# Nearest 2x upsampling: the first 52 rows of every partition taken from a block of their own in DRAM

## The chip, the core and the metric

The kernel runs on one core of a Trainium2 chip. The metric is the device time of one execution in microseconds. Before the change the median of three runs is 197.23 us (197.15 to 197.36).

## What is computed

The input `x` is float32 of shape (16, 64, 64, 64). Every value is written four times: each row of 64 becomes a row of 128 by doubling every element, and each of these rows is written twice.

```
for i in range(new_h):
    for j in range(new_w):
        result[:, :, i, j] = x[:, :, i // scale_factor, j // scale_factor]
```

No arithmetic takes place. 16.78 MB come in and 67.11 MB go out, 83.89 MB in all.

## The kernel before

**Rows.** The three leading dimensions are taken together: 65,536 rows of 64 floats (256 B). Each of the 128 partitions has 512 of them, one after another in DRAM (`xp`, L173), so that partition p starts 128 KiB after partition p-1. The output is cut in the same way: an input row makes 256 floats (1 KiB), and a partition has 512 KiB (`op`, L174).

**Memory.** One buffer `mem` (L187) holds everything: in each partition a free stretch of 79 x 256 floats, and behind it the 512 rows of the input (`xt`). The expanded groups of rows are written by turns at the start of the buffer and at a place that ends in the rows of `xt` already used (L208).

**Loads.** Four transfers on SyncE's queue (L195) bring rows 0 to 32, 32 to 256, 256 to 480 and 480 to 512 of every partition. They are the first instructions of SyncE, moved ahead of the start barrier by `begin_before_barrier`, and wait for nothing. Call them load 0 to load 3.

**Groups.** The rows are worked on in nine groups of 52, 40, 52, 63, 52, 64, 63, 63 and 63 rows (L181). Of each group VectorE copies 9/16 (L215) and ScalarE the rest (L216), both with an input pattern that repeats every element and every row. Then SyncE issues one store for the group (L217). Call them store 0 to store 8. VectorE's part of the first group is rows 0 to 29, ScalarE's is rows 29 to 52; load 0 therefore serves VectorE alone, and ScalarE waits for load 1.

**What sets the order.** All 13 transfers go through one queue, in the order in which SyncE issues them. Store 0 has an extra wait by hand: for load 2 (`loads[-2]`, L221), so that the stores begin as the loads end, while load 3 still runs. From the third group on a group's copies wait until the store two before it has left its place in `mem`.

`close_early` rewrites the end of the program, so that SyncE's last instruction is the wait for the last store.

Of the kernel before, what the change touches and what calls it, by code (L numbers as in the profile page):

```python
# [153 lines left out]
@with_exitstack  # L154
def kernel(
    ctx: ExitStack,
    tc: tile.TileContext,
    x: bass.AP,
    scale_factor: int,
    out: bass.AP,  # L160
):
    nc = tc.nc
    nc.at_finalize(begin_before_barrier)
    nc.at_finalize(close_early)
    P = nc.NUM_PARTITIONS
    s = int(scale_factor)
    B, C, H, W = x.shape
    R = B * C * H // P
    fdt = x.dtype

    xp = x.rearrange("b c h w -> (b c h) w").rearrange("(p r) w -> p r w", p=P)  # L173
    op = out.rearrange("b c (h hd) w -> (b c h) (hd w)", hd=s).rearrange(  # L174
        "(p r) w -> p r w", p=P
    )

    rows = [52, 40, 52, 63, 52, 64, 63, 63, 63]  # L181
    GROW = s * s
    FREE = 79
    WF = FREE * GROW * W
    assert sum(rows) == R
    mem_pool = ctx.enter_context(tc.tile_pool(name="mem", bufs=1))
    mem = mem_pool.tile([P, WF + R * W], fdt, name="mem")  # L187
    xt = mem[:, WF:].rearrange("p (r w) -> p r w", r=R)

    HEAD = 32
    cuts = [0, HEAD, R // 2, R - 32, R]
    loads = [
        nc.sync.dma_start(out=xt[:, lo:hi], in_=xp[:, lo:hi])  # L195
        for lo, hi in zip(cuts, cuts[1:])
    ]

    def expanded(r0, r1):
        return (  # L200
            xt[:, r0:r1].unsqueeze(2).unsqueeze(4).to_broadcast([P, r1 - r0, s, W, s])
        )

    r0 = 0
    before = (0, 0)
    for n, k in enumerate(rows):
        size = k * GROW * W
        at = 0 if n % 2 == 0 else WF + r0 * W - size  # L208
        assert at >= before[1] or at + size <= before[0]
        before = (at, at + size)  # L210
        u = mem[:, at : at + size].rearrange(
            "p (k a w b) -> p k a w b", k=k, a=s, w=W
        )
        kv = k * 9 // 16
        nc.vector.tensor_copy(out=u[:, :kv], in_=expanded(r0, r0 + kv))  # L215
        nc.scalar.copy(out=u[:, kv:], in_=expanded(r0 + kv, r0 + k))  # L216
        store = nc.sync.dma_start(out=op[:, r0 : r0 + k, :], in_=u)  # L217
        if n == 0:
            tc.add_manual_dep(
                store.ins,  # L220
                loads[-2].ins.name,  # L221
                mybir.DependencyInfo(
                    mybir.DependencyClass.Sync, mybir.DependencyReason.DATA
                ),
                reason="stores begin as the loads end",
            )
        r0 += k
# [35 lines left out]
```

## Time and profile before

| what | value |
|---|---|
| median of three runs | 197.23 us |
| the profiled execution, its own time | 197.0 us |
| its span, first to last instruction | 195.7 us |
| outside the span | 1.3 us |
| transfers | 13, in 1872 packets |
| VectorE busy | 69.7 us (36%) |
| ScalarE busy | 51.4 us (26%) |
| load 0 landed, by VectorE's first copy | 4.59 us |
| load 1 landed, by its second copy | 21.52 us |
| load 2 landed, by the chain | 38.44 us |

The span is counted from SyncE's first instruction. A transfer is cut into packets, and 16 DMA engines move them at the same time; the DMA share is the mean busy share of these engines. A short window's GB/s is rough, since whole packets are put where they start.

In the views "mem<-in_x_dram" is a load, "out_dram<-mem" a store, "mem<-mem" a copy, SPq is SyncE's queue, and "L215" is a line of the kernel.

### The profile page before, as it was taken

What the parts mean: (1) busy time and instruction counts of PE and PEld (TensorE: products, weight loads), DVE (VectorE), ACT (ScalarE), POOL (GpSimd) and SP (SyncE); (2) the same over time, 40 slices, a digit from 0 to 9 for tenths busy, and PEclk for the clock granted to TensorE, in tenths of its full rate; (3) what the DMA queues carried; (4) which work ended last, traced back from release to release, by engine and by line L of the source; (5) the groups of instructions that cost most, each with busy time, mean ns of one, the idle gap of its engine ahead of it and who ended that gap; (6) DMA issues with size and microseconds to landing.
All of it is one profiled execution on the core that took longest, in us unless ns stands there. A gap on an engine that the chain in (4) does not pass through costs nothing.

```text
span 195.7 us, 105 instructions
## 1 busy us (share of the span) xinstructions
DVE 69.7 (36%) x9; ACT 51.4 (26%) x10; POOL 0.2 (0%) x4
## 2 busy tenths in 40 slices
DVE  0950600000039299069008205930692079100000
ACT  0000595000036093064910006666000074000000
POOL 0000000000000000000000000000000000000000
DMA  9899889799899989899999899999999999999994
GB/s 402 375 481 457 375 375 563 310 440 523 348 442 452 526 348 512 359 422 422 422 422 523 348 523 429 429 429 429 422 422 422 422 422 422 528 514 422 435 422 211
DMA packets 1872, 83.89 MB, mean 429 GB/s; under 512 B 208, under 2 KB 208, under 8 KB 208
## 3 DMA queue, kind: packets, MB, share of 16 engines
q1 hardware_dynamic: 1872, 83.89, 99.3%
HBM read 16.78 MB, written 67.11 MB: 429 GB/s over the span
## 4 chain that ended last, share of the span: by engine, by line
DMA 67%; DVE 18%; SPq 0%; issue 0%; DVEq 0%
DMA out_dram<-mem 48%; DMA mem<-in_x_dram 19%; DVE mem L215 18%; SPq L195 0%; DVEq L215 0%; SPq L217 0%
## 5 line engine op out<-in xcount | busy, mean ns | idle before, releaser
L215 DVE COPY mem<-mem 128x8960 f32<-128x8960 f32 (+3 forms) x9 | 69.7, 7740 | 97.5 <-DMA out_dram<-mem 83.9
L216 ACT COPY mem<-mem 128x7168 f32<-128x7168 f32 (+2 forms) x9 | 50.1, 5572 | 90.8 <-DMA out_dram<-mem 84.3
L216 ACT ACT_TABLE_LOAD x1 | 1.3, 1283 | 21.6 <-DMA mem<-in_x_dram 21.6
L244 POOL MEMSET const-bfloat16-1.0<- 128x1 bf16 x1 | 0.1, 102 | 0.0
L244 POOL MEMSET const-uint8-127<- 128x1 uint8 x1 | 0.1, 102 | 0.0
L244 POOL MEMSET const-float32-0.0<- 128x1 f32 x1 | 0.1, 99 | 0.2 <-issue 0.2
L244 POOL MEMSET const-float32-1.0<- 128x1 f32 x1 | 0.1, 99 | 0.0
## 6 DMA issues: line engine op xcount, KB each, us to landing
out_dram<-mem SPq DMA_DIRECT2D x4, 8064.0 KB, 28.4
out_dram<-mem SPq DMA_DIRECT2D x3, 6656.0 KB, 19.7
mem<-in_x_dram SPq DMA_DIRECT2D x2, 7168.0 KB, 29.3
out_dram<-mem SPq DMA_DIRECT2D x1, 5120.0 KB, 29.8
mem<-in_x_dram SPq DMA_DIRECT2D x2, 1024.0 KB, 22.1
out_dram<-mem SPq DMA_DIRECT2D x1, 29.9
```

Of the source, the lines that this page charges most:

```text
L215: nc.vector.tensor_copy(out=u[:, :kv], in_=expanded(r0, r0 + kv))
L216: nc.scalar.copy(out=u[:, kv:], in_=expanded(r0 + kv, r0 + k))
L244: nc = _bacc.Bacc("TRN2", target_bir_lowering=False, num_devices=1)
```

## The change

Input and output are each cut into two blocks. The first block is the first 128 x 52 rows of `x` (1.70 MB in one piece), 52 for each partition; the second is the rest, 460 rows for each partition. A partition's rows 0 to 52 now come from the first block and its rows 52 to 512 from the second, and the output is cut alike. Load 0 brings 52 rows instead of 32, and load 1 204 instead of 224.

```diff
-    xp = x.rearrange("b c h w -> (b c h) w").rearrange("(p r) w -> p r w", p=P)
-    op = out.rearrange("b c (h hd) w -> (b c h) (hd w)", hd=s).rearrange(
-        "(p r) w -> p r w", p=P
-    )
+    HEAD = 52
+    xf = x.rearrange("b c h w -> (b c h) w")
+    of = out.rearrange("b c (h hd) w -> (b c h) (hd w)", hd=s)
+
+    def blocks(flat):
+        return (
+            flat[: P * HEAD].rearrange("(p r) w -> p r w", p=P),
+            flat[P * HEAD :].rearrange("(p r) w -> p r w", p=P),
+        )
+
+    def rows_of(parts, lo, hi):
+        if hi <= HEAD:
+            return parts[0][:, lo:hi]
+        assert lo >= HEAD
+        return parts[1][:, lo - HEAD : hi - HEAD]
+
+    xp, op = blocks(xf), blocks(of)
...
-    HEAD = 32
     cuts = [0, HEAD, R // 2, R - 32, R]
     loads = [
-        nc.sync.dma_start(out=xt[:, lo:hi], in_=xp[:, lo:hi])
+        nc.sync.dma_start(out=xt[:, lo:hi], in_=rows_of(xp, lo, hi))
         for lo, hi in zip(cuts, cuts[1:])
     ]
...
-        store = nc.sync.dma_start(out=op[:, r0 : r0 + k, :], in_=u)
+        store = nc.sync.dma_start(out=rows_of(op, r0, r0 + k), in_=u)
```

The distance from one partition's rows to the next partition's changes thus:

| | before | first block | second block |
|---|---|---|---|
| input | 131,072 B | 13,312 B | 117,760 B |
| output | 524,288 B | 53,248 B | 471,040 B |

A row of load 0 or of store 0 now ends where the next partition's begins. The nine groups, the copies, the place of each group in `mem` and the wait of store 0 for load 2 stay.

## Prediction

> **What bounds the kernel now.** I began with the page's first three parts, to see who is busy. VectorE works 36% of the span and ScalarE 26%, and the DMA engines never rest:
>
> ```profile
> DMA  9899889799899989899999899999999999999994
> ...
> DMA packets 1872, 83.89 MB, mean 429 GB/s; under 512 B 208, under 2 KB 208, under 8 KB 208
> ## 3 DMA queue, kind: packets, MB, share of 16 engines
> q1 hardware_dynamic: 1872, 83.89, 99.3%
> ```
>
> The reader is to see the 99.3%: the 16 engines are occupied for all of the span but about 1.4 us of 195.7. The same view, asked for the stretch from 1.02 us (the first packet) to 195.28 us (the last packet's end), says where that rest lies:
>
> ```profile
> q1 hardware_dynamic: 1872, 83.89, 100.0%
> ```
>
> So there is no gap inside: 1.02 us pass before the first packet and 0.4 us after the last. That also says how to read the chain that ended last, which names VectorE for 18%:
>
> ```profile
> 0.91 37.52 DMA mem<-in_x_dram
> ...
> 38.52 18.23 DMA out_dram<-mem
> ...
> 56.85 7.90 DVE mem L215
> ...
> 64.83 19.72 DMA out_dram<-mem
> ```
>
> The chain follows one transfer at a time. While VectorE copies from 56.85 to 64.75 us, store 1, which was queued behind store 0, keeps the engines at work; the copies are covered. What counts is bytes by pace, and so I read the pace in windows (the last column is GB/s):
>
> ```profile
> 0.90:3.90 3.00, 0.00 (x0) 0.00 (x0) 0.00 (x0) 1.00 0.98 347
> 3.90:20.90 17.00, 7.88 (x1) 0.00 (x0) 0.00 (x0) 1.00 1.01 436
> 20.90:37.90 17.00, 3.09 (x1) 10.41 (x3) 0.00 (x0) 1.00 1.00 432
> 119.30:157.60 38.30, 18.97 (x2) 12.31 (x2) 0.00 (x0) 1.00 1.00 434
> ```
>
> Two things matter here. Loads, whose partitions lie 128 KiB apart, go at 434 GB/s (mean of 436 and 432); stores, whose partitions lie 512 KiB apart, go at 434 too. A fourfold distance and the opposite direction give one pace, so neither sets it. And only the first 3 us are slower, at 347.
>
> At 434 GB/s one input row of all 128 partitions (32,768 B) takes 0.0755 us and its output row (131,072 B) 0.302 us. 512 of both make 193.3 us. The other 2.4 us of the span are the start and the end: 1.02 before the first packet, 0.4 after the last, and some 0.5 in the first load (0.60 us by the window, 3.00 x 87/434, of which 0.12 lie before 1.02 us; by single packet records, the 128 packets of load 0 last 368 ns in the mean and the equal packets of load 3 last 310, so 8 per engine x 58 ns = 0.47). What is left, 0.5 us or 0.3%, is about as much as windows of this kind are rough by.
>
> **The change, part by part.**
>
> *Load 0 grows from 32 to 52 rows.* It landed at 4.59 us; 20 rows more at 0.0755 are 1.51, so 6.1 us. VectorE's first copy (7.88 us) then runs from 6.1 to 14.0 instead of 4.6 to 12.5. Its next copy waits for load 1, which ends with row 256 in both kernels and so lands at 21.5 as before: 7.5 us of cover are left. On the path: 0. If load 1 came before 14.0, the delay would show in VectorE, and still not at store 0, see next.
>
> *ScalarE's first copy needs load 0 only.* It waited 21.6 us for load 1. Now its table load (1.28) and copy (5.10) run from 6.1 to 12.5, and its second copy (4.03) from 21.5 to 25.5, where the old pair ended at 32.0. That takes 6.5 us off ScalarE's work ahead of stores 0 and 1. SyncE held store 0 for another reason:
>
> ```profile
> SPq L217 <- DMA mem<-in_x_dram: 36.1, 1, 36.1
> ```
>
> This is the hand-made wait for load 2, which ended at 38.44, 6.4 us after ScalarE was done. The slack grows to 12.9 us and is worth 0. What covers the issue of store 0 at 38.52 is load 3, whose 32 rows keep the engines busy for 2.4 us; that row range and its place in the queue are unchanged.
>
> *Load 1 shrinks from 224 to 204 rows.* The sum of loads 0 and 1 is 256 rows in both. Transfers stay 13, and if each keeps 128 pieces (1872 less 208 small packets is 1664, 13 x 128), the packet costs stay. 0.
>
> *No wait is added*, no queue is passed by another, and stores 1 to 8 keep their order and their buffers. The tightest cover afterwards is that of store 2, issued at 64.8 while store 1 lands at about 68.8: 4 us. 0, unless a store gets slower by that.
>
> *The distances change.* This is the only part that can touch the path, and the trace shows no transfer with the new distances. Bounds:
> - Steady pace, gain side: 0, since engines that are 100.0% busy move 434 GB/s in both directions at two distances, which is a ceiling of theirs and not of an address pattern.
> - Steady pace, loss side: the slowest pace in the trace, 347 GB/s, for the block that lies in one piece. Load 0 (1.70 MB): 4.91 against 3.93 us, +0.98, less the 0.60 that is paid now, so +0.4. Store 0 (6.82 MB): 19.6 against 15.7, +3.9. Together +4.3. I take 0, from the rows nearest by far: 34 us of loads and 38 us of stores without a slow stretch.
> - Start of load 0: the 0.47 us lie mostly in the first packet of each engine (728 ns against 309 over the first 16 packets). Gain at most 0.47, if 16 engines that start together hinder each other because of the 128 KiB distance. Loss 0.29, if the excess grows with the bytes (0.47 x 20/32). I take -0.1: it sits in the first packet and so is mostly waiting for first data, which another distance doesn't remove.
>
> **A rule against the trace.** The Trainium skill, page "DMA: Bandwidth & Descriptors", section "Latency and other measured facts", speaks for the change: copies between DRAM tensors whose rows lie 512 KiB apart gave 207 GB/s per direction, and an uneven distance 214. An estimate by it takes 3.3% off the stores' 154.6 us, so -5.1 us. The stores' row above, 434 GB/s at 512 KiB, disagrees, and the same page's "Where 436 GB/s comes from" gives 435 as the ceiling of the ports. I go by the row.
>
> **Sum.** 195.7 - 0.1 = 195.6 us of span; with 1.3 outside, 196.9 for the profiled execution. That execution (197.0) lay 0.23 under the median, so the forecast for the median is 197.23 - 0.1 = **197.1 us**. A measurement of this kernel can tell about 0.2%, 0.39 us, from no change.
>
> **The rivals.**
> 1. *The block in one piece has a slower pace.* Sixteen engines that read or write rows 13 or 52 KB apart work in one small stretch of DRAM, and may hinder each other there. For: the only slow stretch of the trace is one where all engines start together in short rows. Against: the last load has the same short rows and isn't slow. Price: +0.4 (load alone) to +4.3 us (with store 0), so 197.6 to 201.5. It decides as soon as the pace over load 0 and store 0 (19.6 us at 434) falls by 2%, below 425 GB/s. Slower.
> 2. *The start gets quick.* The 0.47 us of the first packets vanish, because the engines no longer begin 128 KiB apart: 196.8 us, 0.24% faster. For: a first packet alone would not take 2.4 times its later time in all 16 engines unless something is shared. Against: waiting for first data needs no collision. More is hardly to be had, for the rest of the span is 100.0% busy at one pace.
> 3. *It doesn't do what it says:* a piece of DRAM without gaps is cut otherwise than into 128 rows, and fewer engines share it. At half of them load 0 and store 0 take 3.9 + 15.7 = 19.6 us more: 216.8 us. Nothing in the profile speaks for it; all 13 transfers of before have 128 pieces, but none of them lay in one piece.
>
> **Chances.** Forecast (within 0.2%) 0.58; rival 1, 0.24; rival 2, 0.14; rival 3, 0.04. So faster 0.14, same 0.58, slower 0.28. The range takes in the forecast and rival 2, hence 196.7 below. Above it may leave out 2 in 10: rival 3 and two thirds of rival 1, hence about a third of the way into its price, +1.3: 198.5.
>
> **What would show it.** In the profile after: VectorE's first copy at 6.1 us, ScalarE's at 7.4 after its table load; the second copies of both at 21.5; store 0 issued at 38.5 behind a wait for load 2; 1872 packets; windows of 434 GB/s from 4 us on. If load 2 lands after 38.6, the loads' pace fell; if store 0 takes more than the 18.23 us from issue to landing, the first block is slow; if load 0 lands at 5.6, rival 2 holds. I am wrong if the pace of a long window departs from 434, in whichever direction: 1% of it is 1.9 us.

## The result and the profile after

The changed kernel takes 197.88 us (197.75 to 197.94) against 197.23 us for the kernel before in the same series: 1.0037 times as long, 95% interval 1.0027 to 1.0048. In a second series (e6 below) it is 1.0041 (1.0029 to 1.0054). Slower, then, by 0.4%; the forecast was no change. In the later series the kernel before takes 197.53 to 197.58 us in the median, 0.3 us more than in this one; a ratio is always taken against the kernel before of the same series.

The profiled execution has a span of 196.5 us and an own time of 197.85 us. Its page, in the lines that answer to those of before:

```profile
DMA  8999999699899999999999899999999999999994
...
DMA packets 1872, 83.89 MB, mean 427 GB/s; under 512 B 208, under 2 KB 208, under 8 KB 208
## 3 DMA queue, kind: packets, MB, share of 16 engines
q1 hardware_dynamic: 1872, 83.89, 99.1%
```

There are as many packets, with as many bytes in all; the engines are still hardly ever idle. The same view for the stretch from the first packet to the last packet's end (1.01 to 196.14 us):

```profile
q1 hardware_dynamic: 1872, 83.89, 99.8%
```

That stretch is 195.1 us long where it was 194.3. By the packet records an engine is busy for 194.8 us of it in the mean, where it was 194.2: 0.6 us of the lengthening are longer packets, and the other 0.3, the step from 100.0% to 99.8%, is time in which some of the 16 engines are not at work. The windows (last column GB/s) and the chain say where to look:

```profile
0.90:3.90 3.00, 0.00 (x0) 1.28 (x1) 0.00 (x0) 1.00 1.00 324
3.90:20.90 17.00, 7.89 (x1) 5.10 (x1) 0.00 (x0) 1.00 1.02 443
20.90:37.90 17.00, 3.09 (x1) 4.03 (x1) 0.00 (x0) 1.00 0.98 426
119.30:157.60 38.30, 18.97 (x2) 12.33 (x2) 0.00 (x0) 1.00 1.00 433
```

```profile
0.89 38.06 DMA mem<-in_x_dram
...
39.05 18.14 DMA out_dram<-mem
...
57.29 7.90 DVE mem L227
...
65.26 19.85 DMA out_dram<-mem
```

The reader is to see that the chain's first transfer took 38.06 us where it took 37.52, and that the first store, which now writes a piece without gaps, took 18.14 where it took 18.23. The loads from 3.9 to 37.9 us keep their mean pace (434.5 against 434), the window of stores goes from 434 to 433 GB/s, and the first 3 us have fallen from 347 to 324. Of the 0.85 us that this span is longer, 0.52 are there by the time load 2 lands (38.96 against 38.44); the other 0.33 come behind it.

SyncE still holds store 0 for load 2 and nothing else:

```profile
SPq L229 <- DMA mem<-in_x_dram: 36.5, 1, 36.5
```

### The profile page after: what moved, and what is told of

Same layout as the page of the kernel before. It is cut to its first block, busy times and chain, and to the rows that moved or that the text cites. A ratio compares the mean times of both kernels' runs of the same rounds, so it can differ in the third digit from the quotient of the medians.

```text
span 196.5 us, 103 instructions
## 1 busy us (share of the span) xinstructions
DVE 69.7 (35%) x9; ACT 51.4 (26%) x10; POOL 0.2 (0%) x4
## 2 busy tenths in 40 slices
DMA packets 1872, 83.89 MB, mean 427 GB/s; under 512 B 208, under 2 KB 208, under 8 KB 208
## 3 DMA queue, kind: packets, MB, share of 16 engines
q1 hardware_dynamic: 1872, 83.89, 99.1%
## 4 chain that ended last, share of the span: by engine, by line
DMA 67%; DVE 18%; SPq 0%; issue 0%; DVEq 0%
DMA out_dram<-mem 48%; DMA mem<-in_x_dram 19%; DVE mem L227 18%; SPq L207 0%; DVEq L227 0%; SPq L229 0%
```

## The experiments

The trace keeps one record for each packet, and for each transfer the moments at which its 16 engines report their share as landed. From these I worked out for load 0 how long after its bytes' need (first packet's start plus 8 packets per engine at their later pace, 159 ns for 4 KiB, 309 for 8 KiB and 498 for 13 KiB) the first and the last engine had landed. Each trace is one execution; the ratios come from 5 to 12 executions of the run.

| run | rows of load 0, bytes between partitions | time over before (95% interval) | load 0 beyond its need, first / last engine, us | load 2 landed, us |
|---|---|---|---|---|
| before | 32, 128 KiB | 1 | 0.81 / 1.07 | 38.44 |
| e5, before again | 32, 128 KiB | 0.9999 (0.9990 to 1.0008) | 0.95 / 1.38 | 38.75 |
| the change | 52, 13 KiB | 1.0037 (1.0027 to 1.0048) | 0.79 / 1.58 | 38.96 |
| e6, the change again | 52, 13 KiB | 1.0041 (1.0029 to 1.0054) | 0.90 / 2.29 | 39.67 |
| e7, input in blocks only | 52, 13 KiB | 1.0041 (1.0028 to 1.0053) | 0.82 / 2.00 | 39.35 |
| e3, output in blocks only | 32, 128 KiB | 1.0003 (0.9994 to 1.0012) | 0.84 / 1.50 | 38.88 |
| e1, longer load 0 only | 52, 128 KiB | 0.9998 (0.9989 to 1.0006) | 0.84 / 1.30 | 38.67 |
| e10, near rows only | 32, 13 KiB | 1.0027 (1.0018 to 1.0037) | 0.72 / 2.34 | 39.68 |
| e13, all but the near rows | 52, 128 KiB | 0.9999 (0.9990 to 1.0007) | 0.87 / 1.20 | 38.56 |
| e9, near rows only | 32, 8 KiB | 0.9986 (0.9978 to 0.9995) | 1.00 / 1.25 | 38.61 |
| e11, near rows only | 32, 12 KiB | 1.0004 (0.9995 to 1.0013) | 0.82 / 1.78 | 39.10 |
| e12, near rows only | 32, 16 KiB | 1.0016 (1.0007 to 1.0024) | 0.77 / 1.78 | 39.13 |
| e18, shorter load 0 only | 16, 128 KiB | 1.0002 (0.9993 to 1.0012) | 0.87 / 1.67 | 39.00 |

The first engine lands 0.7 to 1.0 us beyond the need everywhere. The last one does so 1.1 to 1.5 us beyond it where 32 or 52 rows lie 128 KiB apart, and 1.6 to 2.3 us where they lie 13 KiB apart.

What follows the last engine's landing of load 0 hardly varies. From there to the landing of load 2 it is 33.84 to 33.90 us in the seven traces with 32 rows and 32.37 to 32.38 in the five with 52; from the landing of load 2 to the end of the span it is 157.2 to 157.6 in all thirteen. So within one execution the time follows the last engine.

One execution, however, need not be typical of a run. e11's trace is of the slowest of its executions (198.02 us against a median of 197.58). e18's is 0.1 us above its median, and its last engine is later than the change's although its rows lie 128 KiB apart and its median costs nothing. What a layout costs is read from the ratios; the traces say where an execution lost it.

**First series: which half of the change?** My first theory was one of size: in the change's trace the first packet of each engine was longer by the same factor as the row (1.6), so a longer load 0 alone would start slowly. Its rival blamed where the rows lie. For the stores, whose 64,512 B packets had gone from 2380 to 2384 ns, I held the output's distance against the engines' being out of step.

e1:

```diff
-    HEAD = 32
+    HEAD = 52
```

> Only load 0 grows to 52 rows; the layout of before stays (partitions 128 KiB apart). Size theory (the first packet of each engine runs at about 89 ns per KiB, so its excess grows with the length of a row of load 0): first-load packets about 589 ns in the mean against 498 at pace, load 2 lands about 0.5 us later than before (38.9 us), the whole about 197.7 us. Address theory (the start is slow because rows lie 13 KB apart): load 2 at 38.5, the whole within 0.15 us of before. For the stores: if the engines' being out of step after a slow start lengthens their packets, the 63-row packets take 2384 ns here too; if the output's distance does, 2380 as before.

Measured: 0.9998, as before. The size theory falls.

e2, the changed kernel:

```diff
-EARLY = 4
+EARLY = 5
-    cuts = [0, HEAD, R // 2, R - 32, R]
+    cuts = [0, 32, HEAD, R // 2, R - 32, R]
```

> The changed layout, but the first block is loaded in two pieces of 32 and 20 rows (one load more, about 0.07 us of packets). Size theory: the start is as before, load 2 lands at 38.5, and only the stores' 0.3 us are left: 197.6 us. Address theory: the start stays slow, load 2 at 39.0, the whole 197.9 us. Store packets of 63 rows: 2384 ns if the output's distance sets it, 2380 if the slow start does and the start is quick here.

Measured: 1.0024 (1.0015 to 1.0033), 198.01 us, load 2 landed at 39.11. With the short first piece the cost stays for the most part: where the rows lie matters.

e3, the changed kernel:

```diff
-    xp, op = blocks(xf), blocks(of)
+    xp, op = xf.rearrange("(p r) w -> p r w", p=P), blocks(of)
...
-        nc.sync.dma_start(out=xt[:, lo:hi], in_=rows_of(xp, lo, hi))
+        nc.sync.dma_start(out=xt[:, lo:hi], in_=xp[:, lo:hi])
...
-    cuts = [0, HEAD, R // 2, R - 32, R]
+    cuts = [0, 32, R // 2, R - 32, R]
```

> The loads and the input's layout of before; only the output is cut into the two blocks (the rows come out in another order than the reference's). If the output's distance of 460 KiB lengthens the store packets: 2384 ns for 63 rows, the whole +0.3 us, 197.55 us. If that came from the slow start: 2380 ns and 197.2 us.

Measured: 1.0003. Stores 460 KiB apart cost nothing that can be measured. (The packets of 64,512 B took 2382 to 2383 ns in the mean of a store, in between the two theories' numbers.)

e4, the kernel before:

```diff
-    HEAD = 32
+    HEAD = 8
```

> The kernel before with a load 0 of 8 rows (2 KiB per partition). Size theory: a first packet of 2 KiB costs a quarter of the excess of one of 8 KiB, 0.1 instead of 0.42 us, so load 2 lands 0.3 us earlier and the whole takes 196.9 us. Address theory, or a fixed wait for first data: no change, 197.2 us. VectorE's first copy then waits for load 1 (21.5 us) and ends by 33, ahead of store 0 at 38.5, so it costs nothing.

Measured: 0.9988 (0.9980 to 0.9997), 197.24 us. That is 0.24 us by the ratio, with an interval that takes in the 0.3 us of the size theory; alone, this run doesn't speak against it. In its trace, though, part of the excess that left load 0 came back in load 1, which took 0.2 us longer than its packets' pace asks for, and e1 had gone against the theory.

**Second series: what is it about the input?** The theory now was that 16 engines hinder each other when they start together in rows that lie near each other; the rival was that any distance that is no power of two is slow.

e6 is the changed kernel once more.

> The changed kernel once more, beside the next three. All theories: 0.3 to 0.5% over before, load 0 landing 0.5 us late, 16 engines 0.8 us apart, store packets of 63 rows at 2384 ns.

Measured: 1.0041. Its chain and VectorE's first copy, which waits for load 0:

```profile
0.89 38.78 DMA mem<-in_x_dram
```

```profile
7.31 7.88 DVE L227 COPY mem<-mem 128x7424 f32<-128x7424 f32 x1 [7.31 <-DMA mem<-in_x_dram]
```

e7, the changed kernel:

```diff
-    xp, op = blocks(xf), blocks(of)
+    xp, op = blocks(xf), of.rearrange("(p r) w -> p r w", p=P)
...
-        store = nc.sync.dma_start(out=rows_of(op, r0, r0 + k), in_=u)
+        store = nc.sync.dma_start(out=op[:, r0 : r0 + k, :], in_=u)
```

> Input cut into the two blocks, output laid out as before (rows come out in another order than the reference's). Input theory (load 0 out of one piece makes a slow start, and the output's distance costs nearly nothing): as slow as the changed kernel, 0.25 to 0.4% over before. Theory of two halves (0.5 us from the start, 0.35 us from longer store packets because of the output's distance): 0.25% over before, and store packets of 63 rows back at 2380 ns. If only input and output together cost: as before.

Measured: 1.0041. All of the cost comes with the input's layout. The store packets of 64,512 B took 2384 to 2387 ns here (means of single stores), although the output lay as before: the output's distance doesn't set them, and the theory of two halves falls.

e8, the changed kernel:

```diff
-        for lo, hi in zip(cuts, cuts[1:])
+        for lo, hi in [(HEAD, R // 2), (0, HEAD), (R // 2, R - 32), (R - 32, R)]
```

> The changed layout with the first two loads exchanged: the engines begin with rows 52 to 256, whose partitions lie 115 KB apart, and the piece without gaps comes second. Both copies of the first group then wait for 21.5 us and end by 33, ahead of store 0. Near-rows theory (16 engines that start together in rows 13 KB apart hinder each other): the start is as quick as before's, the engines end load 1 within 0.3 us of each other, and the whole is back within 0.15% of before. Odd-distance theory (any distance that is no power of two makes the start slow): as slow as the changed kernel.

Measured: 1.0015 (1.0006 to 1.0024). Neither: less than half of the cost is left when the engines begin 115 KiB apart, but not nothing, and in the trace the engines end this first transfer 0.73 us apart.

e9, the kernel before:

```diff
+    xh = x.rearrange("b c h w -> (b c h) w")[: P * HEAD].rearrange(
+        "(p r) w -> p r w", p=P
+    )
...
-        nc.sync.dma_start(out=xt[:, lo:hi], in_=xp[:, lo:hi])
+        nc.sync.dma_start(out=xt[:, lo:hi], in_=xh if lo == 0 else xp[:, lo:hi])
```

> The kernel before, but load 0 (32 rows per partition) reads the first 128 x 32 rows of x in one piece, 8 KiB from partition to partition; these are other rows than the reference's for this place. Near-rows theory: the start is slow here too, 0.2 to 0.3% over before, although the distance is a power of two and the load is small. Odd-distance theory, or a theory that it takes all of the change: within 0.1% of before.

Measured: 0.9986 (0.9978 to 0.9995). The nearest rows of all, in one piece, are quicker than rows 128 KiB apart. The near-rows theory falls.

**Third series: the distance alone.** Load 0 keeps its 32 rows and everything else its place; only the distance of the rows that it reads is varied. e5 is the kernel before once more.

> The kernel before once more, for a second trace of it beside the next three. Load 0 ends for the slowest engine 0.7 to 1.0 us later than its bytes need, store packets at 1966 and 2380 ns without excess. Whole equal to before.

e10 (in e11 `48` and in e12 `64` stand for `52`), against e9:

```diff
-    xh = x.rearrange("b c h w -> (b c h) w")[: P * HEAD].rearrange(
+    xh = x.rearrange("b c h w -> (b c h) w")[: P * 52].rearrange(
         "(p r) w -> p r w", p=P
-    )
+    )[:, :HEAD]
```

> The kernel before, but load 0 (32 rows per partition, as before) reads rows that start 13 KiB apart from partition to partition, other rows than the reference's for this place; all later loads and all stores as before. Distance theory (rows that start at odd KiB make 16 engines begin slowly and out of step): the slowest engine ends load 0 1.2 us or more late instead of 0.7 to 0.9, store packets get longer by 3 to 5 ns although no store was changed, 0.2 to 0.4% over before. Theory that the longer load 0 or the 115 KB rows of load 1 are needed for it: as before.

> As the run with 13 KiB, but rows 12 KiB apart. If starts off a 4 KiB boundary make it slow: quick here, within 0.1% of before. If every distance that is no power of two does: slow as with 13 KiB, 0.2 to 0.4% over before.

> As the run with 13 KiB, but rows 16 KiB apart, a power of two. Both distance theories: quick, like the run with 8 KiB, 0 to 0.15% under before, engines in step within 0.3 us. If gaps between the rows that are read matter instead: slow like 13 KiB, which has gaps as well.

Measured: e5 0.9999, e10 (13 KiB) 1.0027, e11 (12 KiB) 1.0004 (0.9995 to 1.0013), e12 (16 KiB) 1.0016 (1.0007 to 1.0024). The two that carry the case are e5 and e10, which load the same number of rows with transfers of the same size. VectorE's first copy and the chain's load of e5:

```profile
4.89 7.89 DVE L215 COPY mem<-mem 128x7424 f32<-128x7424 f32 x1 [4.89 <-DMA mem<-in_x_dram]
```

```profile
0.90 37.84 DMA mem<-in_x_dram
```

and of e10:

```profile
5.85 7.89 DVE L218 COPY mem<-mem 128x7424 f32<-128x7424 f32 x1 [5.85 <-DMA mem<-in_x_dram]
```

```profile
0.89 38.79 DMA mem<-in_x_dram
```

Load 0 lands 0.96 us later, load 2 is 0.95 us longer on its way, and the spans differ by 0.99 (197.1 against 196.2): what is lost in load 0 is lost for good. e10's profiled execution is one of its slowest (198.48 us against a median of 198.17), so these traces show where the time goes; what it comes to is 0.6 us between the medians. e10's store packets of 64,512 B took 2384 to 2386 ns in the mean of a store, e5's 2380 to 2381, with the same stores. So they lengthen with the addresses of load 0, though no store was touched. e11 and e12 agree with no simple rule: 16 KiB, a power of two, is slow; 12 KiB isn't, in the median, though its executions spread widely (spans of 196.0 to 196.7 us).

**Fourth series: is that all of it?** Open was whether the rest of the change costs something once load 0 starts as before.

e13, the changed kernel:

```diff
     xp, op = blocks(xf), blocks(of)
+    xw = xf.rearrange("(p r) w -> p r w", p=P)
...
-        nc.sync.dma_start(out=xt[:, lo:hi], in_=rows_of(xp, lo, hi))
+        nc.sync.dma_start(out=xt[:, lo:hi], in_=xw[:, lo:hi] if lo == 0 else rows_of(xp, lo, hi))
```

> The changed kernel in all but one place: load 0 (52 rows) reads rows 128 KiB apart, as before, which are other rows than the reference's for this place. If all of the cost lies in the addresses of load 0: within 0.1% of before, and store packets with 0 to 2 ns excess although the stores' distance is that of the changed kernel. If the other distances cost as well: 0.15 to 0.3% over before.

Measured: 0.9999 (0.9990 to 1.0007). VectorE's first copy and the chain's load:

```profile
6.21 7.88 DVE L228 COPY mem<-mem 128x7424 f32<-128x7424 f32 x1 [6.21 <-DMA mem<-in_x_dram]
```

```profile
0.89 37.67 DMA mem<-in_x_dram
```

Against e6, with the same 52 rows and the same later loads and stores, load 0 lands 1.1 us earlier and load 2 takes 1.1 us less (the kernel before takes 197.54 and 197.55 us in these two series). So the cost of the change lies in the addresses from which load 0 reads, and what the rest of it costs is under 0.1%.

e14 is e4 with `HEAD = 4`. e15, the changed kernel:

```diff
-    HEAD = 52
+    HEAD = 32
-    rows = [52, 40, 52, 63, 52, 64, 63, 63, 63]
+    rows = [32, 40, 47, 61, 47, 57, 57, 57, 57, 57]
```

e16, the changed kernel:

```diff
-EARLY = 4
+EARLY = 5
-    cuts = [0, HEAD, R // 2, R - 32, R]
+    cuts = [0, 8, HEAD, R // 2, R - 32, R]
```

> The kernel before with a load 0 of 4 rows (1 KiB per partition). If a short first piece wakes the engines cheaply: 0.1 to 0.2% under before, like the run with 8 rows. If the 8 rows were a fluke of that series: within 0.05% of before.

> The change's idea with a first block of 32 rows per partition: 8 KiB apart, the other 480 rows 120 KiB apart; groups of 32, 40, 47, 61, 47 and five of 57 rows, so one store more (0.07 us of packets). If 8 KiB apart in one piece makes a quick start also here: 0.1% under before to equal. If a block in one piece is slow whatever its distance: 0.2 to 0.4% over before.

> The changed kernel with load 0 cut into 8 and 44 rows (one load more, 0.07 us of packets). If the length of the first packets matters in this layout: half of the cost gone, 0.1 to 0.25% over before. If only where they lie matters: 0.3 to 0.45% over before, as the changed kernel.

Measured: e14 0.9995 (0.9986 to 1.0004); e15 1.0003 (0.9994 to 1.0012), one store more included; e16 1.0021 (1.0013 to 1.0030). A block in one piece isn't slow by itself: with 8 KiB between its rows it costs nothing. And a short first piece from the 13 KiB block doesn't cure it.

**Fifth series: does a short load 0 beat both kernels?** e17 is e4 once more, e18 the same with `HEAD = 16`.

> The kernel before with a load 0 of 8 rows, in another series. If a short first piece helps: 0.05 to 0.2% under before again. If not: within 0.05%.

> The kernel before with a load 0 of 16 rows (4 KiB per partition). If a short first piece helps: between before and the run with 8 rows, 0 to 0.1% under before. If not: within 0.05%.

Measured: e17 197.11 us in the median against 197.58 for the kernel before, but 0.9997 with an interval of 0.9975 to 1.0019, too wide to tell: nine of its eleven executions lie below that median, but one took 199.31 us. e18: 1.0002 (0.9993 to 1.0012). Over the four runs with a short load 0, only e4's interval lies below 1, and that narrowly. Whether 8 rows are a tenth or two better stays open.

## Why the prediction was wrong

**The step that failed** is "Start of load 0": "Gain at most 0.47 [...]. Loss 0.29 [...]. I take -0.1: it sits in the first packet and so is mostly waiting for first data, which another distance doesn't remove." For the first engine that holds: it lands load 0 0.7 to 1.0 us beyond its need, whatever the distance. But I priced the start by a mean over 16 engines, and the end is set by the last one. In the trace of before the last engine was 0.26 us behind the first, and I did not look at that spread; the change makes it 0.8 (1.4 in e6). The term that I put at -0.1 measured +0.51: the last engine's landing went from 1.07 to 1.58 us beyond its need, and nothing behind it made this good. The mean that I used, the excess by packets, can't tell a slow run from another: it is 0.47 us in the trace of before, 0.68 in e5, 0.73 in the change and 0.65 in e10, while the last engine's is 1.07, 1.38, 1.58 and 2.34. The loss bound of 0.29, by the number of bytes, was therefore not a bound: the cost does not go by the bytes (e1), it goes by where the first rows lie.

**Ceiling of the steady pace: right.** Loads and stores of the changed distances run at 433 to 434 GB/s; e3 and e13 put the price of all distances behind load 0 at nothing that can be measured. What I did not foresee is the small lengthening of the store packets by 3 to 7 ns out of 2380 in the mean of a store. It comes with the slow start (e7, e10) and sums up to 0.3 to 0.5 us for an engine in the mean. How much of it reaches the time differs by trace: from load 2's landing to the end of the span the trace of before takes 157.2 us, e5 157.4, the change 157.6, e6 157.5, e10 157.5, e13 157.6. Against the trace of before that is 0.33 us of the change's 0.85, against e5 0.15; and e13 takes as long without longer packets and costs nothing.

**Load 0 and ScalarE: right where it counts.** The copies ahead of the stores, from the timelines (start, length, engine and line, and in brackets the idle time before and who ended it). In the kernel before:

```profile
4.59 7.88 DVE L215 COPY mem<-mem 128x7424 f32<-128x7424 f32 x1 [4.59 <-DMA mem<-in_x_dram]
21.52 3.09 DVE L215 COPY mem<-mem 128x5632 f32<-128x5632 f32 x1 [9.04 <-DMA mem<-in_x_dram]
21.57 1.28 ACT L216 ACT_TABLE_LOAD   x1 [21.57 <-DMA mem<-in_x_dram]
```

In the changed kernel:

```profile
2.49 1.28 ACT L228 ACT_TABLE_LOAD   x1 [2.49 <-PEq L256]
6.60 5.10 ACT L228 COPY mem<-mem 128x5888 f32<-128x5888 f32 x1 [2.83 <-DMA mem<-in_x_dram]
6.60 7.89 DVE L227 COPY mem<-mem 128x7424 f32<-128x7424 f32 x1 [6.60 <-DMA mem<-in_x_dram]
22.03 3.09 DVE L227 COPY mem<-mem 128x5632 f32<-128x5632 f32 x1 [7.54 <-DMA mem<-in_x_dram]
22.11 4.03 ACT L228 COPY mem<-mem 128x4608 f32<-128x4608 f32 x1 [10.42 <-DMA mem<-in_x_dram]
39.05 129.28 SPq L229 DMA_DIRECT2D out_dram<-mem  x9
```

Forecast for VectorE's first copy was 6.1 us, and it began at 6.60; the 0.5 is the start. ScalarE's table load didn't wait for load 0 as I had said, but ran at 2.49 us, so that its copy began at 6.60 with VectorE's and not 1.3 us later. Both then sat idle for 7.5 and 10.4 us before load 1, and were done by 26.1, 13 us ahead of store 0.

**Load 1, waits, buffers, packets: right.** 1872 packets; second copies at 22.0 and 22.1, later by the start alone; store 0 waits for load 2 only.

**Rival 1** had the sign, and the time falls into its price, but not for its reason; that the range, 196.7 to 198.5, holds the measured time is therefore luck. The pace inside the block is unhurt: packets of load 0 after an engine's first took 498 ns with few exceptions, their full pace, and store 0 took 18.14 us from issue to landing. e15 shows a block in one piece at no cost. **Rival 2** had the place, and the opposite sign.

**The rule that was weighed.** The Trainium skill, "DMA: Bandwidth & Descriptors", section "Latency and other measured facts", gives 207 GB/s for copies between DRAM tensors with rows 512 KiB apart; its 214 belongs to a distance of 4 MiB and 4 KiB, and 4 MiB and 192 B gave 97, so it doesn't say that uneven is faster as such. For the stores here neither is faster (e3, 460 against 512 KiB, 1.0003), and at the start an uneven 13 KiB is slower than 128 KiB. The same section gives 0.2 us as the mean and 2 us under high load for an access to HBM; the first packets here lasted up to 1.5 us beyond their pace (1599 ns against 498 in the changed kernel at its longest, 2001 in e7), which lies in that span, but no run shows what delays them.

**What stays open** is which property of the addresses makes the last engine late. With 32 rows in load 0, 8 KiB is quick (0.9986), 12 KiB and 128 KiB are level, 16 KiB (1.0016) and 13 KiB (1.0027) are slow. Being near, being in one piece, being a power of two and lying on a 4 KiB boundary are each contradicted by one of these runs. 115 KiB for a first load of 204 rows (e8, 1.0015) lies in between. In e6, e7 and e10 four of the 16 engines land load 0 1.7 to 2.3 us beyond the need and the other twelve by 1.5; which engines these are the packet records don't say, and no run moved the place where `x` begins.

## What to carry to other kernels

Where, as here, 16 DMA engines work from the first microsecond to the last, what one of them loses at the start isn't made up, and what counts is when the slowest engine lands its share of the first transfer: read the spread between the engines at the first landing, not a mean over them. Changing the layout of a tensor also changes which addresses all engines touch first. When a layout is to be tried, put it on the first transfer alone and then on all but the first; two runs then say more than the whole does. And where the cost is some tenths of a per cent, let the ratios of many executions decide, and one trace only say where to look.

## What the runs showed of the hardware that was not expected

- Engines that start out of step stay so for long: in e6 they were 1.40 us apart at the landing of load 0, still 1.37 us at the end of load 3, 35 us later, and 1.1 us at the last store.
- In traces with late starters the store packets of 64,512 B take 2384 to 2386 ns in the mean (single ones mostly 2380 to 2389), in the others 2380 to 2381, for the same stores (e10 against e5); e3 lies between. e18 shows it with rows 128 KiB apart. In e4 the engines were 0.7 us apart at store 0 without this, so the spread alone doesn't explain it.
- The length of load 0's rows (8 or 13 KiB) makes no difference with 128 KiB between the partitions (e1, 0.9998).
